# The second layer's ConvFFN in two phases: up by seven of eight quarter products, gated values through DRAM, down summed in PSUM

## The chip, the cores and the metric

One core of one Trainium2 chip. The metric is the device time of one execution in microseconds, the median of several runs. The engines are named as in the profile: PE is TensorE (matmul), DVE is VectorE, ACT is ScalarE, POOL is GpSimd, SP is SyncE, which issues most of the transfers.

## What is computed

A diffusion backbone of two layers over 1024 latent tokens and 256 context tokens, width 1024. Layer 0 mixes by differential attention and a Fourier mixer, layer 1 by Mamba-2 SSD and S5; every layer ends with a gated ConvFFN and a post-norm. The change is in the ConvFFN of layer 1, which works on the 1024 latent tokens alone. Cut from the reference:

```python
D_MODEL, SEQ, D_FF, CONV_K = 1024, 1024, 2816, 3
def conv_ffn(u, w_up, b_up, conv_w, conv_b, w_down, b_down):
    hdn = dwconv_centered(u @ w_up + b_up, conv_w, conv_b)   # 3 taps along the tokens
    val, gate = jnp.split(hdn, 2, axis=-1)
    return (val * jax.nn.silu(gate)) @ w_down + b_down
def post_norm_layer(h, y_mix, mods, ln_g, ln_b, ffn):
    h = layer_norm(ALPHA * h + mods[2][:, None] * y_mix, ln_g[0], ln_b[0])
    f = conv_ffn(modulate(h, mods[3], mods[4]), *ffn)
    return layer_norm(ALPHA * h + mods[5][:, None] * f, ln_g[1], ln_b[1])
```

## The kernel before

Every float32 operand of a matmul is split into a high part `h` (ACT, a copy into the fp32r type) and a low part `l` = value - high (DVE). A product of two operands takes three matmuls: high by high, high by low, low by high. `uh` and `ul` are the parts of the modulated input, channels on partitions, all 1024 tokens wide, made tile by tile by the output projection `out_proj` (L1304) that ends layer 1's mixer (`ul` at L372).

The hidden channels are worked on in NFB = 22 blocks `fb` of 128, each with a value half and a gate half (`conv_ffn`, L1466). Per block, PE does 2 halves x 2 token chunks x 8 k-blocks x 3 = 96 up matmuls of 128x512 (`up_mul`, L1426, into banks `mm`). ACT copies each bank with the bias into a padded row buffer `hb` (L1520). The convolution is one ACT instruction for the middle tap (L1540) and two DVE instructions for the outer ones (L1541, L1542), 1024 wide. Gating is a silu on ACT (L1546), a product on DVE (L1548) and the split of the result (L1552, L1554).

The down product runs one block behind: while PE does block `fb`'s gate half, the 48 down matmuls (L1561) of block fb - 1 are woven in, three up and three down in turn. Each group of three fills a bank (`tr` or `bg`), for one tile of 128 tokens and one half of the output width, and a DVE addition (L1575) adds the bank to `y` in SBUF: 16 additions per block. The down weights are multiplied by the residual gate on POOL when they arrive (L1500). The last three blocks' down products (`hold` = 3) are left to the tail: nine matmuls per bank, added by L2621, followed by the layer norm of each tile (L2609 to L2650) and the store of the output.

All of this is written out by hand in program order; each engine's queue is in that order. `FirstBlock` (L1430) reads the first block's weights ahead, and its product is begun inside `out_proj`. Loads of weights are issued by SP, two halves ahead (L1488, L1498). Beside it, POOL makes the residual from `yacc`, which stays in SBUF (L2582 to L2592).

## Time and profile before

| | |
|---|---|
| median of 3 runs | 3225.18 us (3224.17 to 3227.72) |
| span of the profiled execution | 3222.3 us |
| mean granted clock of TensorE in it | 0.978 |
| busy in the span: PE / DVE / ACT / POOL | 3056.3 / 2197.5 / 1207.7 / 743.2 us |
| layer 1's ConvFFN in it | from about 2431 us to the end |

The profile page gives, for one profiled execution, the busy time of each engine, the span in 40 slices, the chain of work that ended last, and the costliest groups of instructions. It names no other time of that execution than its span, from the first to the last instruction. Of the trace behind it, the windows give the same sums for any stretch, the timeline gives single instructions, and the chain of waits shows at each moment which work the end was waiting for.

### The profile page before, as it was taken

To read this page: it belongs to the slowest core of one execution; us is meant where nothing else is said; L and a number is where in the kernel's file an instruction comes from. 1 tells how busy PE (TensorE), PEld (TensorE's weight loads), DVE (VectorE), ACT (ScalarE), POOL (GpSimd) and SP (SyncE) were. 2 spreads that over 40 slices of the span, in tenths; PEclk is the share of its full clock that TensorE was granted. 3 is DMA by queue.
4 is the path that set the end of the run, shared out by engine and by line. 5 is a ranking of instruction groups with operands and counts; after the bars stand their busy time and mean duration, and the time that the engine had idled before them with its cause. 6 is when DMAs were issued, how large, how long until landed. Compare 5 with 4: busy or idle time off the path is not lost.

```text
span 3222.3 us, 39551 instructions
## 1 busy us (share of the span) xinstructions
PE 3056.3 (95%) x15416; PEld 2464.6 (76%) x15416; DVE 2197.5 (68%) x3214; ACT 1207.7 (37%) x2022; POOL 743.2 (23%) x639
## 2 busy tenths in 40 slices
PE   8999989999999999999999799997798999999997
PEld 4777779998888778877878577876487777777775
DVE  2288768886566565566666866759886667666667
ACT  3411258784522222222222452444354232232334
POOL 1056412221000000002430522216635301010013
PEclk9999999999999999999999899998899999999998
DMA  8635666613322222222321323320312121111111
GB/s 274 211 107 172 193 172 162 153 33 129 131 79 79 73 67 91 79 79 79 115 94 53 107 87 106 87 68 1 130 53 72 40 66 46 40 53 46 40 60 58
DMA packets 269614, 304.82 MB, mean 95 GB/s; under 512 B 22439, under 2 KB 206165, under 8 KB 269428
## 3 DMA queue, kind: packets, MB, share of 16 engines
q1 hardware_dynamic: 256452, 263.98, 26.8%
q0 software_dynamic: 6912, 23.11, 2.1%
q10 hardware_dynamic: 6064, 15.21, 1.6%
q8 instruction: 121, 1.98, 0.3%
q14 instruction: 65, 0.53, 0.1%
HBM read 237.48 MB, written 58.47 MB: 92 GB/s over the span
## 4 chain that ended last, share of the span: by engine, by line
PE 74%; DVE 16%; DMA 4%; ACT 3%; issue 2%; SPq 0%; POOL 0%; ACTq 0%; DVEq 0%; POOLq 0%
PE mm L1428 30%; PE tr L1561 10%; PE mm L1353 6%; PE bg L1561 5%; PE mm L2288 4%; PE s L1094 3%; PE mm L978 3%; PE mm L878 3%; PE bg L1152 3%; DVE cv L1542 2%; PE bg L266 1%; DVE cv L1541 1%; PE bg L1131 1%; PE tr L352 1%; PE bg L1817 1%
## 5 line engine op out<-in xcount | busy, mean ns | idle before, releaser
L1428 PE MATMUL mm<-uh,wusl 128*128 128x512 f32 (+1 forms) x1768 | 653.7, 370 | 7.6 <-DVE wusl L90 7.6
L1428 PE MATMUL mm<-uh,wush 128*128 128x512 f32 (+1 forms) x1768 | 655.4, 371 | 3.5 <-ACT wush L89 3.5
L1428 PE MATMUL mm<-ul,wush 128*128 128x512 f32 (+1 forms) x1768 | 654.6, 370 | 0.2 <-DVE ul L372 0.2
L1520 ACT ACTIVATE hb<-mm,ffc 128x512 f32<-128x512 f32 (+1 forms) x220 | 141.0, 641 | 975.3 <-PE mm L1428 975.2
L1575 DVE TENSOR_TENSOR y<-y,tr 128x512 f32<-128x512 f32 x469 | 317.4, 684 | 250.3 <-PE tr L1561 249.5
L1428 PEld LDWEIGHTS mm<-uh,wush 128*128 128x128 f32 x1768 | 333.8, 189 | 90.1 <-issue 23.6
L1428 PEld LDWEIGHTS mm<-uh,wusl 128*128 128x128 f32 x1768 | 333.8, 189 | 66.6 <-DVE wusl L90 10.2
L1428 PEld LDWEIGHTS mm<-ul,wush 128*128 128x128 f32 x1768 | 333.6, 189 | 64.7 <-DVE ul L372 0.4
L1575 DVE TENSOR_TENSOR y<-y,bg 128x512 f32<-128x512 f32 x235 | 160.8, 684 | 139.7 <-PE bg L1561 139.6
L1561 PE MATMUL tr<-wdsh,gh 128*128 128x512 f32 x516 | 209.0, 405 | 20.5 <-DVE y L1575 15.1
L1561 PE MATMUL tr<-wdsl,gh 128*128 128x512 f32 x516 | 204.4, 396 | 4.0 <-DVE wdsl L90 4.0
L1561 PE MATMUL tr<-wdsh,gl 128*128 128x512 f32 x516 | 205.8, 399 | 0.0
L1500 POOL TENSOR_TENSOR wdf<-wdf,g 128x1024 f32<-128x1024 f32 x22 | 68.4, 3108 | 573.9 <-DMA wdf<-in_ffn_w_down_dram 356.9
L1102 DVE TENSOR_REDUCE mx<-s 128x1 f32<-128x1280 f32 x120 | 150.6, 1273 | 47.7 <-PE s L1094 47.7
L1541 DVE SCALAR_TENSOR_TENSOR cv<-hb,ffc,cv 128x1282 f32<-128x1282 f32 (+3 forms) x91 | 134.4, 1477 | 48.1 <-ACT cv L1540 47.9
L1542 DVE SCALAR_TENSOR_TENSOR cv<-hb,ffc,cv 128x1282 f32<-128x1282 f32 (+3 forms) x91 | 163.8, 1800 | 3.5
L1659 POOL DMA_DIRECT2D g<-in_ln_g_dram x1 | 0.6, 599 | 623.0 <-DVE y L1575 623.0
L90 DVE TENSOR_TENSOR wusl<-wuf,wush 128x1024 fp32r<-128x1024 f32 x86 | 117.4, 1365 | 25.5 <-ACT wush L89 25.1
L1107 ACT ACTIVATE p<-s,mx 128x1280 f32<-128x1280 f32 x96 | 127.8, 1331 | 18.2 <-DVE r L1112 12.7
L1561 PEld LDWEIGHTS tr<-wdsh,gh 128*128 128x128 f32 x516 | 98.0, 190 | 47.8 <-DVE y L1575 22.8
L978 PE MATMUL mm<-uh,wsh 128*128 128x512 f32 (+1 forms) x320 | 124.8, 390 | 0.0
L1152 PE MATMUL bg<-vt,wt 128*128 128x128 f32 x960 | 124.5, 276 | 0.0
(694 smaller groups left out, 6720.3 us busy)
## 6 DMA issues: line engine op xcount, KB each, us to landing
wuf<-in_ffn_w_up_dram SPq DMA_DIRECT2D x88, 512.0 KB
adaw<-in_ada_w_dram SPq DMA_DIRECT2D x40, 1024.0 KB
wdf<-in_ffn_w_down_dram SPq DMA_DIRECT2D x44, 512.0 KB
wf<-in_attn_w_in_dram SPq DMA_DIRECT2D x18, 512.0 KB
adaw<-in_ada_w_dram SPq DMA_DIRECT2D x16, 512.0 KB
tq<-qd SPq DMA_DIRECT2D x24, 320.0 KB
t1k<-kd SPq DMA_DIRECT2D x24, 320.0 KB
t2k<-kd SPq DMA_DIRECT2D x24, 320.0 KB
```

The costliest lines, as they stand in the source:

```text
L978: T.matmul(pt.rearrange("p (t n) -> p t n", n=P), lhsT=w_[:, k, :], rhs=u_[:, o // P:(o + n) // P, k, :], start=(k + i == 0), stop=(k == K ...
L1102: V.reduce_max(t.mx[:, i, q:q + 1], t.s[i][:, c0:c0 + nk], axis=X, negate=True)
L1107: S.activation(t.p[i][q], t.s[i][:, c0:c0 + nk], AF.Exp, bias=t.mx[:, i, q:q + 1], accum_out=t.sm[:, i, q:q + 1])
L1152: T.matmul(t.po[:, P:2 * P], lhsT=t.wt[0][:, b, :], rhs=vt[:, b, :], start=(b == 0), stop=(b == NTT - 1))
L1353: T.matmul(pt, lhsT=u_[:, k, :], rhs=w_[k][:, hc], start=(k + i == 0), stop=(k == K - 1 and i == 2))
L1428: T.matmul(pt, lhsT=w_[:, k, :], rhs=u_[:, k, o:o + n], start=(k + j == 0), stop=(k == KB - 1 and j == 2))
L1520: S.activation(hb[vi][:, pos(o):pos(o) + n], pt[:, :n], AF.Identity, bias=ffc[l][:, 0, blk(b):blk(b) + 1])
L1541: V.scalar_tensor_tensor(out=c, in0=hb[vi][:, lo:hi], scalar=fc[:, 2], in1=c, op0=ALU.mult, op1=ALU.add)
L1542: V.scalar_tensor_tensor(out=c, in0=hb[vi][:, lo + 2:hi + 2], scalar=fc[:, 4], in1=c, op0=ALU.mult, op1=ALU.add)
L1561: T.matmul(pt, lhsT=g_[:, c0:c0 + P], rhs=w_[:, hc], start=(start and j == 0), stop=(stop and j == 2))
L1575: V.tensor_tensor(out=yacc[ti][:, hc], in0=yacc[ti][:, hc], in1=pt, op=ALU.add)
L2288: T.matmul(pt[0:M, :n], lhsT=w_[:, k, :], rhs=u_[:, k, o:o + n], start=(k + i == 0), stop=(k == KB - 1 and i == len(pairs) - 1))
```

## The change

Only layer 1's ConvFFN and its neighbours change; layer 0 still uses `conv_ffn`.

**Up phase** (`lat_up`). For one block of channels the up product is seen as a 2 x 2 matrix of quarters: rows are the value and the gate half of the weights, the inner index the two halves of the 1024 input channels, columns the two halves of the tokens. `a11` to `a22` are the quarters of the weights, `b11` to `b22` those of the input. Instead of eight quarter products (12 matmuls each) seven are made, in Winograd's form, from `s1` to `s4` (sums of weight quarters, made per block on DVE) and `t1` to `t4` (sums of input quarters, made once by `gen_sums`, t1 in the place of b12). Part of the recombination happens in PSUM, where a bank is read by ACT (`snap`) and then accumulated further, part by four DVE additions from PSUM into `hb` (`add`). Blocks 0 and 1 are still made plainly, with 96 matmuls each, while `gen_sums` works; the 20 others take 84. The gated values are not split: they are stored to DRAM as float32 (`g1_d`, 512 KB per block) from POOL's queue.

**Down phase** (`Down`). It begins when the up phase has ended. Four tiles of tokens by two halves fill all eight PSUM banks and all 22 blocks are accumulated there; then the same for the other four tiles. A step of this loop (one block, one group) is 24 matmuls. For each step SP loads the gated values (256 KB) and the down weights (512 KB, now read twice in all and not multiplied by the gate), two steps staged; ACT and DVE split both into one of five operand slots. At the end of a group the last three blocks are done bank by bank, and `tile_done` multiplies the bank by the gate, adds it to the residual and runs the layer norm. The normed stream `z` that the residual needs is stored to DRAM by `out_proj` and read back on POOL's queue; POOL makes the residual during the down phase.

Layer 1's `FirstPair` takes the place of `FirstBlock` (value and gate weights of block 0, split on POOL). The matmuls of this ConvFFN are 2 x 96 + 20 x 84 + 1056 = 2928, and were 22 x 96 + 1056 = 3168.

```diff
+    class FirstPair:
...
+        def product(self, ci, uh, ul):
+            o, n = self.chunks[ci]
+            pt = pp.tile([P, 512], F32, name='mm', bufs=4)
+            self.pts.append(pt)
+            for j, nm in enumerate(('a11', 'a12')):
+                quarter(pt[:, :n], self.hl[nm], [t[:, 4 * j:4 * j + 4, o:o + n] for t in (uh, ul)], j == 0, j == 1)
+
+    def quarter(pt, w, u, start, stop, step=lambda: None):
+        for k in range(4):
+            for j, (w_, u_) in enumerate(((w[0], u[0]), (w[0], u[1]), (w[1], u[0]))):
+                T.matmul(pt, lhsT=w_[:, k, :], rhs=u_[:, k, :], start=start and k + j == 0, stop=stop and k == 3 and (j == 2), skip_group_check=True)
+            step()
+
+    def lat_up(l, uh, ul, c0, pre, g_d, gq, plain, dpool, ones_ahead):
...
+        def summed(n, nm):
+            if n < NFB and n not in plain:
+                x, y, f = {'s1': ('a21', 'a22', ALU.add), 's2': ('s1', 'a11', ALU.subtract), 's3': ('a11', 'a21', ALU.subtract), 's4': ('a12', 's2', ALU.subtract)}[nm]
+                A[n, nm] = rpool.tile([P, 4, P], F32, name='s', bufs=3)
+                V.tensor_tensor(out=A[n, nm], in0=src(n, x), in1=src(n, y), op=f)
...
+        def gated(n):
+            if n >= 0:
+                V.tensor_tensor(out=cv[n, 0], in0=cv[n, 0], in1=cv.pop((n, 1)), op=ALU.mult)
+                gq(out=g_d[n], in_=cv.pop((n, 0)))
...
+        for n in range(len(plain), NFB):
...
+            X, Wb, Y, Z = [bank() for _ in range(4)]
+            quarter(X, w['a11'], U['b11'], True, True)
+            snap(n, 0, 0, X)
+            hi(m, 'a11')
+            silu(n - 1)
+            load(n + 2)
+            quarter(Wb, w['a12'], U['b21'], True, True)
+            lo(m, 'a11')
+            gated(n - 1)
+            summed(m, 's1')
+            hi(m, 'a12')
+            add(0, 0, Wb)
+            quarter(X, w['s2'], U['t2'], False, True)
...
+            snap(n, 0, 1, X)
...
+            quarter(Y, w['s1'], U['t1'], True, True)
...
+            snap(n, 1, 1, Y)
...
+            quarter(X, w['s3'], U['t3'], False, True)
...
+            snap(n, 1, 0, X)
+            hi(m, 's3')
+            add(1, 1, X)
...
+            quarter(Y, w['s4'], U['b22'], False, True)
+            lo(m, 's3')
+            add(0, 1, Y)
+            hi(m, 's4')
+            tap(n, 0)
...
+            quarter(Z, w['a22'], U['t4'], True, True)
+            lo(m, 's4')
+            conv(n, 0)
+            hi(m, 'a22')
+            add(1, 0, Z)
+            tap(n, 1)
+            lo(m, 'a22')
+            conv(n, 1)
...
+    class Down:
...
+        def load(self):
...
+                s = self.st[q] = [self.pool.tile([P, D], F32, name='wdf', bufs=2), self.pool.tile([P, 512], F32, name='gf', bufs=2)]
+                dma(out=s[1][:, :nt * P], in_=self.g_d[fb][:, t0 * P:(t0 + nt) * P])
+                dma(out=s[0], in_=a['ffn_w_down'][self.l, fb * P:(fb + 1) * P, :])
...
+        def run(self, bank, tile_done, step=lambda: None):
+            q = 0
+            for gi, (t0, nt) in enumerate(self.groups):
+                pts = [bank(i) for i in range(2 * nt)]
+                for fb in range(NFB - self.hold):
+                    for i in range(2 * nt):
+                        self.mul(pts[i], q, i // 2, i % 2, fb == 0, False)
+                        if i == 0 and self.ns < q + len(self.slots):
+                            self.load()
+                            self.split()
+                        step()
+                    q += 1
+                for i in range(2 * nt):
+                    for h in range(self.hold):
+                        self.mul(pts[i], q + h, i // 2, i % 2, False, h == self.hold - 1)
...
+                    tile_done(t0 + i // 2, i % 2, pts[i])
+                q += self.hold
...
-    out_proj(1, list(range(2, NTT)), NCTX, None, load_h2, (woh, wol), uh, ul, m3s, m3b, None, scale_g, None, pre, early, own=yacc)
+    out_proj(1, list(range(2, NTT)), NCTX, None, load_h2, (woh, wol), uh, ul, m3s, m3b, z_d, scale_g, None, pre, early, own=yacc)
...
-        conv_ffn(1, uh, ul, 8, [(0, 512), (512, 512)], [(0, 1024, 1)], yacc, pA, pB, pre, 3, fold=gate, bg=gen_res1(), nbg=9, dbank=dbank, ends=ends, begin=start)
+        dn = Down(1, g1_d, [(0, 4), (4, 4)], 3)
...
+        starter, finish_up, left = lat_up(1, uh, ul, 0, pre, g1_d, nc.gpsimd.dma_start, (0, 1), dpool, None)
+        finish_up()
...
+        dn.slots += [(p2, i) for i in range(2, 5)]
...
+        def tile_done(ti, half, pt):
+            h, hc = (hs[ti], slice(half * 512, half * 512 + 512))
+            V.tensor_tensor(out=pt, in0=pt, in1=gate[:, hc], op=ALU.mult)
+            V.scalar_tensor_tensor(out=h[:, hc], in0=h[:, hc], scalar=1.0, in1=pt, op0=ALU.mult, op1=ALU.add, accum_out=st2[half][:, ti:ti + 1])
```

How the queues change. PE in the middle of the ConvFFN, before: up products (`mm`) and down products (`tr`, `bg`) in turn, the down bank waiting for the DVE addition that frees it.

```order
L1428 MATMUL mm<-uh,wush 128x512
L1428 MATMUL mm<-ul,wush 128x512
L1428 MATMUL mm<-uh,wusl 128x512
L1561 MATMUL tr<-wdsh,gh 128x512 [waits DVE_49]
L1561 MATMUL tr<-wdsl,gh 128x512
L1561 MATMUL tr<-wdsh,gl 128x512
L1428 MATMUL mm<-uh,wush 128x512
```

And now, in a short block, where the third quarter product ends and the fourth begins (L1478 is `quarter`; `t2h` is the high part of t2):

```order
L1478 MATMUL mm<-t2h,s2h 128x512
L1478 MATMUL mm<-t2l,s2h 128x512
L1478 MATMUL mm<-t2h,s2l 128x512
L1478 MATMUL mm<-uh,s1h 128x512 [waits DVE_49]
L1478 MATMUL mm<-ul,s1h 128x512
L1478 MATMUL mm<-uh,s1l 128x512
L1478 MATMUL mm<-uh,s1h 128x512
```

No down product stands between them, and the only wait is at the head of a quarter.

DVE in a block before (`y` additions, the convolution `cv`, the split of weights):

```order
L1548 TENSOR_TENSOR cv_22261<-cv_22261,cv_22382 128x1024 [waits Activation_49]
L1554 TENSOR_TENSOR gl<-cv_22261,gh 128x1024 [waits Activation_49]
L90 TENSOR_TENSOR wusl<-wuf,wush 128x1024 [waits DMAHW3_49,Activation_49]
L1575 TENSOR_TENSOR y_18199<-y_18199,tr 128x512 [waits PE_49] x2
L1575 TENSOR_TENSOR y_18200<-y_18200,bg 128x512 [waits PE_49]
L1541 SCALAR_TENSOR_TENSOR cv_22478<-hb_20292,ffc_101,cv_22478 128x1024 [waits Activation_49]
L1542 SCALAR_TENSOR_TENSOR cv_22478<-hb_20292,ffc_101,cv_22478 128x1024 [waits DVE_49]
```

And now, in a short block (`s1l` to `s4l` are low parts of the next block's sums, `hbv` and `hbg` the row buffers, L1562 the additions from PSUM, L1544 the convolution):

```order
L1534 TENSOR_TENSOR s1l<-s,s1h 128x512 [waits PE_49,Activation_49]
L1522 TENSOR_TENSOR s<-wuv,s 128x512 [waits DVE_49]
L1562 TENSOR_TENSOR hbg<-hbg,mm 128x512 [waits Activation_49]
L1534 TENSOR_TENSOR s3l<-s,s3h 128x512 [waits PE_49,Activation_49]
L1562 TENSOR_TENSOR hbv<-hbv,mm 128x512 [waits PE_49]
L1534 TENSOR_TENSOR s4l<-s,s4h 128x512 [waits Activation_49]
L1544 SCALAR_TENSOR_TENSOR cvv<-hbv,ffc_101,cvv 128x1024 [waits DMASW7_49,Activation_49]
L1544 SCALAR_TENSOR_TENSOR cvv<-hbv,ffc_101,cvv 128x1024 [waits DVE_49]
L1562 TENSOR_TENSOR hbg<-hbg,mm 128x512 [waits PE_49]
L1534 TENSOR_TENSOR a22l<-wug,a22h 128x512 [waits Activation_49]
L1544 SCALAR_TENSOR_TENSOR cvg<-hbg,ffc_101,cvg 128x1024 [waits Activation_49]
L1544 SCALAR_TENSOR_TENSOR cvg<-hbg,ffc_101,cvg 128x1024 [waits DVE_49]
```

The additions into `y` are gone; each block has small instructions for the next block's operands between those for its own recombination.

DVE in the second plain block, in the middle of `gen_sums` (`xb`, `xt`, `t4l` are its work; `s1l` and `a22l` here are the low parts of that block's gate weights):

```order
L1589 TENSOR_TENSOR t4l<-xb_20474,t4h 128x512 [waits Activation_49]
L1574 TENSOR_TENSOR xb_20496<-uh,ul 128x512
L1574 TENSOR_TENSOR xb_20501<-uh,ul 128x512 [waits DVE_49]
L1577 TENSOR_TENSOR xt_20503<-xb_20501,xb_20496 128x512 [waits DVE_49]
L1574 TENSOR_TENSOR xb_20509<-uh,ul 128x512
L1534 TENSOR_TENSOR s1l<-wug,s1h 128x512 [waits DMAHW4_49,PE_49,Activation_49]
L1534 TENSOR_TENSOR a22l<-wug,a22h 128x512 [waits PE_49,Activation_49]
L1544 SCALAR_TENSOR_TENSOR cvg<-hbg,ffc_101,cvg 128x1024 [waits Pool_49]
L1544 SCALAR_TENSOR_TENSOR cvg<-hbg,ffc_101,cvg 128x1024 [waits DVE_49,Pool_49]
```

`s1l` is the 42nd instruction of DVE after the last `ul` of the output projection; PE's gate half of the second plain block (L1478, `mm<-uh,s1l`) waits for it.

## Rows read from the trace of the kernel before

**Rows 1.** The page: busy time of each engine, and GB/s in 40 slices of the span.

```profile
PE 3056.3 (95%) x15416; PEld 2464.6 (76%) x15416; DVE 2197.5 (68%) x3214; ACT 1207.7 (37%) x2022; POOL 743.2 (23%) x639
...
GB/s 274 211 107 172 193 172 162 153 33 129 131 79 79 73 67 91 79 79 79 115 94 53 107 87 106 87 68 1 130 53 72 40 66 46 40 53 46 40 60 58
```

**Rows 2.** Windows: stretch, length, busy us (instructions) PE, PEld, DVE, ACT, POOL; PEclk, DMA share, GB/s.

```profile
2345.00:2440.00 95.00, 94.36 (x466) 77.45 (x465) 76.01 (x166) 52.86 (x108) 40.02 (x18) 1.00 0.19 64
...
2700.00:2800.00 100.00, 97.69 (x423) 78.79 (x422) 68.52 (x73) 28.79 (x32) 9.94 (x3) 1.00 0.15 48
3160.00:3222.00 62.00, 40.88 (x166) 32.03 (x164) 52.09 (x128) 26.31 (x35) 24.14 (x10) 0.84 0.17 68
```

**Rows 3.** Chain of waits, late and at the last block: start us, us, what.

```profile
2692.84 3.30 DVE cv L1542
...
3101.96 3.29 DVE cv L1542
...
3119.40 21.80 PE mm L1428 x96
```

**Rows 4.** Timeline of PE: alternating products, then after an idle time.

```profile
2703.16 0.39 PE L1428 MATMUL mm<-uh,wush 128*128 128x512 f32 x1
...
2704.55 0.39 PE L1428 MATMUL mm<-uh,wush 128*128 128x512 f32 x1
...
2473.27 0.80 PE L1428 MATMUL mm<-uh,wusl 128*128 128x512 f32 x1 [3.24 <-DVE wusl L90]
...
2480.57 0.63 PE L1428 MATMUL mm<-ul,wush 128*128 128x512 f32 x1
2480.99 0.63 PE L1428 MATMUL mm<-uh,wusl 128*128 128x512 f32 x1
```

**Rows 5.** Timeline of DVE from 2709 to 2734: start us, us, what.

```profile
2712.95 1.28 DVE L1542 SCALAR_TENSOR_TENSOR cv<-hb,ffc,cv 128x1024 f32<-128x1024 f32 x1
2715.36 1.23 DVE L1548 TENSOR_TENSOR cv<-cv,cv 128x1024 f32<-128x1024 f32 x1 [1.13 <-ACT cv L1546]
...
2727.29 3.29 DVE L1542 SCALAR_TENSOR_TENSOR cv<-hb,ffc,cv 128x1024 f32<-128x1024 f32 x1
2730.51 0.67 DVE L1575 TENSOR_TENSOR y<-y,tr 128x512 f32<-128x512 f32 x1
2731.11 0.68 DVE L1575 TENSOR_TENSOR y<-y,bg 128x512 f32<-128x512 f32 x1
```

**Rows 6.** Timeline of POOL, same stretch.

```profile
2726.18 3.33 POOL L1500 TENSOR_TENSOR wdf<-wdf,g 128x1024 f32<-128x1024 f32 x1 [31.13 <-DVE y L1575]
```

**Rows 7.** Groups by line from 2400 to the end: count, busy us, mean ns, idle before.

```profile
L1575 DVE TENSOR_TENSOR y<-y,tr 128x512 f32<-128x512 f32 x203 | 136.1, 682 | 94.1 <-PE tr L1561 94.1
...
L1561 PE MATMUL tr<-wdsh,gh 128*128 128x512 f32 x236 | 97.7, 414 | 20.5 <-DVE y L1575 15.1 <-DVE y L2621 5.5
...
L1520 ACT ACTIVATE hb<-mm,ffc 128x512 f32<-128x512 f32 x88 | 60.2, 685 | 408.9 <-PE mm L1428 408.9
```

**Rows 8.** Timeline of DVE in the last 60 us.

```profile
3200.35 0.20 DVE L2630 TENSOR_SCALAR tst<-tst,tst 128x1 f32<-128x1 f32 x1
...
3205.49 0.20 DVE L2630 TENSOR_SCALAR tst<-tst,tst 128x1 f32<-128x1 f32 x1
...
3209.21 0.08 DVE L2621 DVE_READ_ACCUMULATOR y<-y,tr 128x1 f32 x1
```

**Rows 9.** Chain of waits at the start of the second ConvFFN.

```profile
2441.90 0.70 DVE ul L372
...
2444.99 10.74 PE mm L1428 x46
```

**Rows 10.** SP's queue, then instructions and landing of tile gl (POOL's queue).

```profile
2720.91 0.57 SPq L1498 DMA_DIRECT2D wdf<-in_ffn_w_down_dram  x1
...
L2576 POOL DMA_DIRECT2D gl<-in_ln_b_dram x1: 536/536/536, 2437.1 to 2437.1; - x1
...
DMA to landing us min/median/max: 4.8/4.8/4.8
```

More of the change, by code (lines that the diff above doesn't have):

```diff
@@ L2547, in load_h2 @@
     def load_h2(t, tt):
+        hc = [slice(0, 512), slice(512, D)]
         if not ln2:
-            ln2.extend([bc_row(pre.pool, a['ln_g'][0, 1:2, :], "wush"), bc_row(pre.pool, a['ln_b'][0, 1:2, :], "wusl")])
-        g2, b2 = ln2
+            for i, rows in enumerate((a['ln_g'], a['ln_b'])):
+                for j in range(2):
+                    ln2.append(pre.pool.tile([P, 512], F32, name=f"a1{j + 1}{'hl'[i]}"))
+                    dma(out=ln2[-1], in_=rows[0, 1:2, hc[j]].broadcast_to([P, 512]))
         dma(out=t, in_=z2_d[tt * P:(tt + 1) * P, :])
-        G.tensor_tensor(out=t, in0=t, in1=g2, op=ALU.mult)
-        G.tensor_tensor(out=t, in0=t, in1=b2, op=ALU.add)
+        for j in range(2):
+            G.tensor_tensor(out=t[:, hc[j]], in0=t[:, hc[j]], in1=ln2[j], op=ALU.mult)
+            G.tensor_tensor(out=t[:, hc[j]], in0=t[:, hc[j]], in1=ln2[2 + j], op=ALU.add)
     def scale_g(ot, tt):
@@ new lines, in body, with dpool, load_z, resid @@
+    g1_d = dp.tile([NFB, P, NLAT], F32, name="g1d")
+    with tc.manual_schedule():
+        dn = Down(1, g1_d, [(0, 4), (4, 4)], 3)
+        def dpool():
+            dn.guard = tc.tile_pool(name="dn1", bufs=1)
+            return dn.start()
+        starter, finish_up, left = lat_up(1, uh, ul, 0, pre, g1_d, nc.gpsimd.dma_start, (0, 1), dpool, None)
+        finish_up()
+        phf.close()
+        ph4.close()
+        dn2 = tc.tile_pool(name="dm1", bufs=1, side="right")
+        p2 = dn2.__enter__()
+        dn.slots += [(p2, i) for i in range(2, 5)]
+        epg = tc.tile_pool(name="ep1", bufs=1, side="right")
+        ep = epg.__enter__()
+        gate, g1, r, g2, b2 = [ep.tile([P, D], F32, name=nm) for nm in ("gate", "g1", "r", "g2", "b2")]
+        for t, src in ((gate, mods_d[1][1:2, 5 * D:6 * D]), (r, a['ffn_b_down'][1:2, :]), (g1, a['ln_g'][1, 0:1, :]), (g2, a['ln_b'][1, 0:1, :]), (b2, a['ln_b'][1, 1:2, :])):
+            nc.gpsimd.dma_start(out=t, in_=src.broadcast_to([P, D]))
+        hs = {}
+        def load_z(t):
+            if t < 8 and t not in hs:
+                hs[t] = ep.tile([P, D], F32, name="z", bufs=5)
+                nc.gpsimd.dma_start(out=hs[t], in_=z_d[(t + 2) * P:(t + 3) * P, :])
+        def resid(t):
+            G.tensor_tensor(out=hs[t], in0=hs[t], in1=g1, op=ALU.mult)
+            yield
+            G.tensor_tensor(out=hs[t], in0=hs[t], in1=r, op=ALU.add)
+            yield
+        def gen_resid():
+            for t in range(5):
+                load_z(t)
+            G.tensor_scalar(gate, gate, IALPHA, None, ALU.mult)
@@ L2594, in gen_res1 @@
-            for t, src in ((g2, a['ln_g'][1, 1:2, :]), (b2, a['ln_b'][1, 1:2, :])):
-                dma(out=t, in_=src.broadcast_to([P, D]))
-                yield
-        first = []
-        ends = {}
-        conv_ffn(1, uh, ul, 8, [(0, 512), (512, 512)], [(0, 1024, 1)], yacc, pA, pB, pre, 3, fold=gate, bg=gen_res1(), nbg=9,
-                 dbank=dbank, ends=ends, begin=start)
-        last = ends['down']
-        junk = pB.tile([P, D], F32, name="wdf")
-        st2 = [pB.tile([P, 8], F32, name=f"tst{i}") for i in range(5)]
+            G.tensor_tensor(out=r, in0=r, in1=g2, op=ALU.add)
@@ L2604, in body @@
+            nc.gpsimd.dma_start(out=g2, in_=a['ln_g'][1, 1:2, :].broadcast_to([P, D]))
+            yield
+            for t in range(5):
+                yield from resid(t)
+        st2 = [ep.tile([P, 8], F32, name=f"tst{i}") for i in range(5)]
         chain = Drip(V)
```

336 lines of the change are left out of this document (282 added, 54 removed).

## The prediction

> **What bounds the kernel now.** I read the page's busy shares first, then the windows by stage, then the chain of waits inside the second layer's ConvFFN, then single instructions. The page says that TensorE is busy for 95% of the span [rows 1]. The window over a steady stretch of this stage says the same more sharply: 97.69 of 100 us, at full granted clock, while VectorE is at 68.52, ScalarE at 28.79, and the transfers move 48 GB/s [rows 2]. So the stage is paced by the number of matmuls times their pitch. The pitch comes from the chain: 96 matmuls in 21.80 us are 0.227 us each [rows 3]. Where up and down products alternate by threes, six starts take 1.39 us, 0.232 each [rows 4].
>
> What lies above that is small. The chain passes through the same long convolution step once per block of channels, at 2692.84 and, 12 blocks later, at 3101.96 [rows 3]: 409.12 / 12 = 34.09 us per block, of which 144 matmuls at 0.2267 us are 32.64. Of the missing 1.45 us a third is the mixed pitch; the rest is the down product's bank that waits for VectorE's add, while VectorE sits in a 3.29 us instruction beside POOL's 3.33 us fold [rows 5, 6]; the same form takes 1.28 us alone [rows 5]. These waits are most of the 15.1 us of idle time that the lines put on the adds [rows 7]. The end is different: in the last 62 us TensorE is busy for 40.88, clock 0.84, and VectorE for 52.09 [rows 2]. There the layer norm of each tile sets the pace, 3205.49 - 3200.35 = 5.14 us per tile [rows 8].
>
> **The change, part by part.** By the listing of instructions nothing differs before the end of layer 1's output projection. From there I go by four stages, on the clock of the span, 3222.3 us; the median of the runs lies 2.9 us above it and I add that at the end.
>
> *Removed.* 240 matmuls (20 blocks of 84 in place of 96), 240 x 0.2267 = 54.4 us of the busiest engine. Also 304 adds of layer 1's down products on VectorE (16 in each of 19 blocks), 0.68 us each [rows 7], and POOL's 22 folds. Most of those adds lay beside matmuls and give nothing directly; the 1.45 us per block goes, but only to be replaced by what is late next.
>
> *Stage 1, two plain blocks.* 192 matmuls, but VectorE must now form t1 to t4. After the last column of the input is there (VectorE's last `ul` ends at 2442.6, the first long run of matmuls starts at 2444.99 [rows 9]) TensorE has 24 matmuls of half width (2.7 us) and 72 whole ones (16.3 us), and reaches the gate half of the second plain block at 2464.0. This half needs `s1l`, the 42nd VectorE instruction from there in the order: 40 of 512 columns at 0.60 us back to back (2730.51 to 2731.11) and two convolution steps at 1.31 (1.28 and the gap to the next) [rows 5]. That is 26.6 us, so 2469.2 with no waits at all; several of them wait for a ScalarE conversion of 0.69 us [rows 7], for which I add 5 us: 2474.4. At 0.69 us apart and with the same handoffs it would be 2478. So TensorE stalls for about 10 us. After an idle 3.24 us the trace shows a pitch of 0.42 us [rows 4] for the 13 recorded matmuls that follow, 13 x 0.20 = 2.6 us lost, so I charge 3.6 after a longer stall. The 72 matmuls left take 16.3, and 1.5 us come from the output projection, where a weight conversion on ScalarE now stands ahead of the last tiles' work (two of its 0.69 us instructions). 2474.4 + 3.6 + 16.3 + 1.5 = **2496** for the start of the 20 short blocks (2484 without the stall, 2500 at the slow end).
>
> *Stage 2, 20 blocks of seven quarter products.* TensorE needs 84 x 0.2267 = 19.04 us, or 19.46 at the mixed pitch of 0.2317. VectorE has 15 instructions of 512 columns (four sums, seven low parts, four adds from PSUM), the gating multiplication (1.23) and four convolution steps (1.31): 15 x 0.62 + 1.23 + 5.24 = 15.8 us busy [rows 5]. It also waits twice for ScalarE, once for the convolution's first tap after the last quarter and once for the silu, 2.7 us together. That is 18.5 of 19.04 us: TensorE still sets the pace, with about 1 us to spare. ScalarE has 11 conversions and snapshots of 0.685 [rows 7] and three of twice the width, under 12 us. The loads are 1 MB of weights and the store 0.5 MB per block, 1.57 MB / 19.4 us = 81 GB/s, against 274 in the first slice of the span [rows 1]. I take 19.4 us: 20 x 19.4 = 388, the stage ends at **2884**. The gated values must be stored before the next block's tap writes the same buffer; the store has some 8 us for that, and a transfer of this size from POOL's queue landed in 4.8 [rows 10].
>
> *Stage 3, the down products.* 1056 matmuls, all accumulated in PSUM, at 0.229 (the middle of both pitches) = 241.8 us. A step is 24 matmuls, 5.5 us. In it VectorE makes two low parts (0.62 + 1.23), ScalarE two high ones, POOL one residual instruction; even the 2 us that POOL added to a VectorE step [rows 5, 6] fits. A step loads 0.79 MB, 143 GB/s, three times the 48 of before [rows 2]. The trace of before has no such steady load here, so I bound it: nothing if the 274 GB/s of the first slice hold [rows 1], 1.6 to 2.6 us per step if the rate stays at 97 to 111 GB/s, as in several slices of before, or each transfer takes what `wdf` took, issued at 2720.91 and used at 2726.18 [rows 6, 10]. I take nothing, since staging runs two steps ahead. Two transitions cost: at the start, 5 rows and 5 tiles (5.2 MB) come in on POOL's queue beside the first steps, and three of five operand slots become free only with the last up matmul, 8 us; between the groups, the eight banks become free only as VectorE finishes each tile (6.3 us per tile, below, against TensorE's 18 x 0.229 = 4.1), 8 us. Each could be 0 to 15.
>
> *Stage 4, the end.* Before, the tail had eight tiles, now four. VectorE does two more instructions of 0.6 us per tile than in the 5.14 us cadence [rows 8], 6.3 us. The last three steps' matmuls (72, 16.5 us) lie inside: 2 + 4 x 6.3 + 13 = 40 us from their first to the end, where 13 is the present distance from the last sum at 3209.2 to 3222.3 [rows 8].
>
> **Sum:** 2884 + (241.8 - 16.5) + 8 + 8 + 40 = 3165.3 against 3222.3, and with 2.9 us outside the span **3168 us**. Beside the 54 us of matmuls the old waits go (21 x 1.45 = 30 us and what the first block lost), and stage 1's stall, the two transitions and the pitch take most of that back.
>
> **The rivals.**
> *VectorE paces stage 2.* Speaking for it: only about 1 us to spare per block, and a chain of handoffs with ScalarE in which each side can be late. If its 512-column instructions take 0.69 (alone) rather than 0.62 and the handoffs 4.7 rather than 2.7 us, a block takes 21.5 us: 20 x 2.1 = 42 us more, **3210**. Against it: in before it drains bursts at 0.60 [rows 5], and POOL, the cause of its long instructions, computes nothing here.
> *No waits at all.* Pitch 0.2267 everywhere, stage 1's stall hidden, 4 us at the transitions: **3134**. For it: steady windows of 98% [rows 2]. Against it: 41 instructions ahead of one that TensorE needs.
> *Loads bound stage 3,* the case on the other side. Mechanism: staging holds two steps, each of two transfers on one queue, and a step's load waits for the split that frees its buffer. At 7.2 to 8.1 us per step in place of 5.5 the 44 steps cost 75 to 114 us, **3243 to 3282**. My forecast has 57 us to give, 57 / 44 = 1.3: it decides from 6.8 us per step, 116 GB/s. For it: no slice of before after the second moves more than 193 GB/s [rows 1]. Against it: low rates of before are low demand, and a load has two steps' time.
> *The stores on POOL's queue are late.* If a store takes 10 us or more and not 4.8, the tap waits, and with it convolution and snapshots: 2.1 us x 20, **3210** as well. The Trainium skill speaks for this one (SBUF — State Buffer, Who interferes with whom): transfers issued from GpSimd can starve while VectorE runs in its two-port modes, and such transfers should go to another queue. By this page the stores of stage 2 would be late and the time near 3210; the page excepts tensor_tensor, the bulk of VectorE's work here. The rows speak against: one from POOL's queue, issued at 2437.1, landed in 4.8 us in a stretch where VectorE was busy for 76.01 of 95 us [rows 2, 10].
>
> **How the numbers follow.** My forecast, 3150 to 3185 around 3168, has 0.66; VectorE's pace 0.15; no waits 0.10; late stores 0.03; loads 0.06. The range 3140 to 3212 leaves out the loads, half of the no-wait case and about half of the two cases near 3210, some 0.2. A measurement can tell about 0.2% (6.5 us) from no change, so faster means under 3218.7: everything but the loads and the upper edge of VectorE's pace. Faster 0.91, the same 0.03, slower 0.06.
>
> **What would show it.** Right: in the steady part of the short blocks TensorE's starts of equal quarters lie 19.0 to 19.6 us apart, with VectorE above 80% busy; a stall of 7 to 12 us at `s1l` in the second plain block, then slow matmuls; 44 steps of 5.4 to 5.6 us with no wait for staging; a hole under 15 us between the groups. Wrong: quarter products that wait for VectorE in every block (first rival), an idle TensorE ended by conversions that follow a transfer in stage 3 (third), taps that wait for the store (fourth), or a boundary between the groups that costs 20 us or more.

## The result, and the profile after

The changed kernel took 3149.9 us (median of 4 runs, 3147.91 to 3151.14) against 3226.45 for the kernel before in the same runs: a ratio of 0.9765, 95% interval 0.9751 to 0.9779. The forecast was 3168 within 3140 to 3212. The profiled execution has a span of 3148.6 us. The head of its page (as in [rows 1]):

```profile
span 3148.6 us, 39836 instructions
...
PE 2989.8 (95%) x15176; PEld 2420.1 (77%) x15176; DVE 2202.4 (70%) x3281; ACT 1277.2 (41%) x2179; POOL 689.7 (22%) x664
```

TensorE is still busy for 95%, but with 66.5 us less work (3056.3 before [rows 1]). The windows by stage (columns as in [rows 2]) are the first 29 us of stage 1, the middle of the short blocks, and the down phase:

```profile
2441.00:2470.00 29.00, 18.47 (x87) 15.00 (x85) 28.05 (x42) 9.60 (x16) 0.00 (x0) 0.87 0.07 19
2700.00:2800.00 100.00, 100.00 (x437) 81.76 (x436) 81.26 (x104) 52.71 (x73) 2.66 (x5) 1.00 0.26 84
2860.00:2960.00 100.00, 95.99 (x413) 78.11 (x412) 71.73 (x48) 36.89 (x45) 45.38 (x26) 0.98 0.63 214
2960.00:3060.00 100.00, 94.99 (x406) 77.41 (x405) 67.28 (x102) 36.60 (x48) 24.62 (x12) 0.97 0.51 170
```

At the start VectorE is at work for 28.05 of 29 us. In the short blocks TensorE is never idle, 100.00 of 100, where it was 97.69 before, and VectorE is at 81.26 instead of 68.52. The transfers, 48 GB/s before in the same stretch [rows 2], are at 84 now, and at 170 to 214 in the down phase. The stages can be read off single starts of TensorE (timeline: start us, us, instruction, idle time before it and its releaser):

```profile
2459.26 0.39 PE L1478 MATMUL mm<-uh,a12l 128*128 128x512 f32 x1
2472.47 0.79 PE L1478 MATMUL mm<-uh,s1h 128*128 128x512 f32 x1 [12.82 <-ACT s1h L1529]
...
2476.02 0.39 PE L1478 MATMUL mm<-uh,s1l 128*128 128x512 f32 x1
...
2496.08 0.39 PE L1478 MATMUL mm<-t2h,s2h 128*128 128x512 f32 x1
...
2862.40 0.39 PE L1478 MATMUL mm<-t2h,s2h 128*128 128x512 f32 x1
...
2876.20 0.39 PE L1766 MATMUL mm<-wdh,gh 128*128 128x512 f32 x1
...
2882.05 0.72 PE L1766 MATMUL mm<-wdh,gh 128*128 128x512 f32 x1 [3.61 <-DVE hbg L1562]
```

*Stage 1.* TensorE reaches the gate half of the second plain block at 2459.5, waits 12.82 us, and works slowly until 2476.02: eight matmuls at a pitch of 0.43 us instead of 0.227, with a granted clock of 0.50 from 2470 to 2475, the lower of its two levels (1.2 of 2.4 GHz). The last 3 us of the wait are ScalarE's: behind a conversion that VectorE's work releases at 2469.41 its queue still holds the copy of a bank and a convolution step, and only then `s1h`, at 2471.80. *Stage 2.* The third quarter product begins at 2496.08 in the first short block and at 2862.40 in the last, so a block takes 366.32 / 19 = 19.28 us. *Stage 3.* The first down matmul starts at 2876.20; after nine matmuls TensorE waits 3.61 us for a bank. From the first short block to the end, these are all its waits (who waits, for whom, us, times, longest):

```profile
PE bg L1766 <- DVE z L2990: 3.7, 2, 1.9
PE mm L1766 <- DVE hbg L1562: 3.6, 1, 3.6
PE tr L1766 <- DVE z L2990: 1.3, 1, 1.3
PE mm L1766 <- DVE wdl L1746: 0.4, 1, 0.4
```

And the chain of waits at the end (start us, us, what; the matmuls, then VectorE at the first bank of the second, third and fourth tile):

```profile
3114.53 6.13 PE mm L1766 x27
3120.68 0.71 DVE mm L2989
...
3126.42 0.62 DVE tr L2989
...
3132.07 0.62 DVE bg L2989
```

It begins with the first 27 of the 72 matmuls that finish the last group. At 2.04 us a bank (9 x 0.227) they would be done at 3114.53 + 16.3 = 3130.9; VectorE follows at 5.7 us per tile (3126.42 - 3120.68, 3132.07 - 3126.42), with the end at 3148.6.

One more reading is needed before runs are compared. The instructions up to this layer's output projection are the same in all of them (in the changed kernel and its variants up to the end of it), yet the last `ul` there starts between 2437 and 2449 us. In the changed kernel it is this row:

```profile
2440.87 0.69 DVE L372 TENSOR_TENSOR ul<-utmp,uh 128x512 fp32r<-128x512 f32 x1 [1.37 <-ACT uh L370]
```

So beside the medians I count from this instruction, the anchor, to the end of the span: 3148.6 - 2440.87 = 707.7 us, and before 3222.3 - 2441.90 = 780.4 [rows 9]. The change is 72.7 us there. This count has a scatter of its own: stretches that a run does not touch still differ by up to 1.9 us between runs (from the first down matmul to the end 271.06 us in e2_sums_half and 272.92 in e1_plain21), partly by the number of slow matmuls after the same wait. I read differences under 2 us as none.

### The profile page after: what moved, and what is told of

It is laid out like the page before. It is cut to its first block, busy times and chain, and to the rows that moved or that the text cites. A ratio compares the mean times of both kernels' runs of the same rounds, so it can differ in the third digit from the quotient of the medians.

```text
span 3148.6 us, 39836 instructions
## 1 busy us (share of the span) xinstructions
PE 2989.8 (95%) x15176; PEld 2420.1 (77%) x15176; DVE 2202.4 (70%) x3281; ACT 1277.2 (41%) x2179; POOL 689.7 (22%) x664
## 4 chain that ended last, share of the span: by engine, by line
PE 75%; DVE 14%; DMA 5%; ACT 3%; issue 2%; SPq 0%; POOL 0%; DVEq 0%; ACTq 0%; POOLq 0%
PE mm L1428 18%; PE mm L1478 13%; PE tr L1902 6%; PE mm L1353 6%; PE mm L2629 4%; PE bg L1902 3%; PE s L1094 3%; PE mm L878 3%; PE mm L1766 3%; PE bg L1152 3%; PE mm L978 2%; PE bg L266 1%; PE bg L1131 1%; PE bg L1766 1%; PE tr L1766 1%
## 5 line engine op out<-in xcount | busy, mean ns | idle before, releaser
L1428 PE MATMUL mm<-uh,wush 128*128 128x512 f32 (+1 forms) x1056 | 378.6, 358 | 0.0
L1428 PE MATMUL mm<-uh,wusl 128*128 128x512 f32 (+1 forms) x1056 | 374.8, 355 | 3.2 <-DVE wusl L90 3.2
L1428 PE MATMUL mm<-ul,wush 128*128 128x512 f32 (+1 forms) x1056 | 375.5, 356 | 0.0
L1916 DVE TENSOR_TENSOR y<-y,tr 128x512 f32<-128x512 f32 x266 | 181.3, 686 | 153.1 <-PE tr L1902 152.3
L1428 PEld LDWEIGHTS mm<-uh,wush 128*128 128x128 f32 x1056 | 199.4, 189 | 57.3 <-issue 23.6
L1428 PEld LDWEIGHTS mm<-ul,wush 128*128 128x128 f32 x1056 | 199.4, 189 | 35.2
L1428 PEld LDWEIGHTS mm<-uh,wusl 128*128 128x128 f32 x1056 | 199.2, 189 | 32.9 <-DVE wusl L90 4.0
L1152 PEld LDWEIGHTS bg<-vt,wt 128*128 128x128 f32 x960 | 116.6, 193 | 0.7
L978 PE MATMUL mm<-ul,wsh 128*128 128x512 f32 (+1 forms) x320 | 115.1, 360 | 0.0
L978 PE MATMUL mm<-uh,wsl 128*128 128x512 f32 (+1 forms) x320 | 114.9, 359 | 0.0
```

The costliest lines, as they stand in the source:

```text
L978: T.matmul(pt.rearrange("p (t n) -> p t n", n=P), lhsT=w_[:, k, :], rhs=u_[:, o // P:(o + n) // P, k, :], start=(k + i == 0), stop=(k == K ...
L1152: T.matmul(t.po[:, P:2 * P], lhsT=t.wt[0][:, b, :], rhs=vt[:, b, :], start=(b == 0), stop=(b == NTT - 1))
L1428: T.matmul(pt, lhsT=w_[:, k, :], rhs=u_[:, k, o:o + n], start=(k + j == 0), stop=(k == KB - 1 and j == 2))
L1916: V.tensor_tensor(out=yacc[ti][:, hc], in0=yacc[ti][:, hc], in1=pt, op=ALU.add)
```

## The experiments

| run | median, us | last `ul` starts | span | from there to the end | against 707.7 |
|---|---|---|---|---|---|
| e1_plain21 | 3200.97 | 2437.01 | 3195.6 | 758.6 | +50.9 |
| e2_sums_half | 3151.16 | 2443.73 | 3151.7 | 708.0 | +0.3 |
| e3_three_plain | 3148.54 | 2443.65 | 3148.3 | 704.7 | -3.0 |
| e4_hold5 | 3147.33 | 2442.18 | 3146.2 | 704.0 | -3.7 |
| e5_dve4 | 3182.72 | 2445.81 | 3182.2 | 736.4 | +28.7 |
| e6_double_load | 3147.59 | 2439.43 | 3147.2 | 707.8 | +0.1 |
| e7_store_sp | 3157.8 | 2442.82 | 3156.5 | 713.7 | +6.0 |
| e8_banks | 3151.58 | 2443.10 | 3151.1 | 708.0 | +0.3 |
| e9_split_first | 3142.84 | 2440.42 | 3139.3 | 698.9 | -8.8 |
| e10_sums_pool | 3158.53 | 2439.63 | 3154.7 | 715.1 | +7.4 |
| e11_all | 3135.7 | 2449.10 | 3141.3 | 692.2 | -15.5 |

**What the seven quarter products are worth.**

```diff
-        ... = lat_up(1, uh, ul, 0, pre, g1_d, nc.gpsimd.dma_start, (0, 1), dpool, None)
+        ... = lat_up(1, uh, ul, 0, pre, g1_d, nc.gpsimd.dma_start, tuple(range(21)), dpool, None)
```

> Two phases without quarter products: 21 blocks of channels made plainly (96 matmuls), only the last with seven quarter products. 19 blocks x 12 = 228 matmuls come back. My theory (the matmul count is what stage 2 is worth, the two phases alone win back the old waits of 1.45 us per block): 228 x 0.2267 = 51.7 us above the changed kernel's 3149.9, so 3198 to 3206, still below 3226. Rival (the seven quarter products bring little because VectorE's sums eat it, and the gain is the phases'): 3150 to 3170. Second rival (the phases bring nothing): 3222 to 3230.

Measured: 3200.97 us (ratio to before 0.9921, 0.9901 to 0.9941), 50.9 us more from the anchor. The 228 matmuls cost 0.223 us each, nearly all of their pitch of 0.227, and the two phases without quarter products are still faster than before. Both rivals fall. The window over its middle shows the plain blocks without any idle time too:

```profile
2600.00:2800.00 200.00, 200.00 (x879) 164.84 (x878) 82.91 (x85) 74.06 (x101) 4.79 (x9) 1.00 0.23 72
```

So the two phases give the part that is not matmuls, about 22 us net of what stage 1 and the transitions cost (2.7 of them are the 12 matmuls that the one short block saves), and the quarter products the rest. In such a window before, TensorE was idle for 2.3 of 100 us [rows 2], with waits for the additions [rows 7]; how much of the 22 us these waits make and how much the mixed pitch, no run separates.

**Stage 1: the stall.** First its order: `gen_sums` advances at every second step only in block 0.

```diff
-            step = lambda: next(sums, None)
+            calls = [0]
+
+            def step():
+                calls[0] += 1
+                if calls[0] > 24 or calls[0] % 2 == 0:
+                    next(sums, None)
```

> The forming of t1 to t4 is stepped half as fast in block 0, so that less of it stands ahead of the second plain block's gate weights; the same work in all. If only the order is at fault, the 12.8 us stall in stage 1 goes with the slow matmuls behind it: 3133 to 3137. If VectorE's amount of work in stage 1 sets the start of the short blocks (53.62 busy of the 60 us from 2440 to 2500), the stall only moves to the first short block: 3146 to 3152. I lean to the second.

Measured: no gain. The stall moved, whole, to the first short block's first weights, as expected:

```profile
2492.24 0.79 PE L1478 MATMUL mm<-uh,a11h 128*128 128x512 f32 x1 [13.28 <-ACT a11h L1529]
...
2497.52 0.62 PE L1478 MATMUL mm<-uh,a12h 128*128 128x512 f32 x1
```

Then more matmuls to cover the same work, three plain blocks (and half the pace up to the 56th step):

> Three plain blocks and t1 to t4 formed at half the pace over them: 12 matmuls more (2.7 us). If VectorE's backlog is what the stall is made of, all of it is hidden now: 12.8 us of stall and about 3.6 us of slow matmuls go, 2.7 come: 3134 to 3138. If the backlog was not the cause (the gate weights' transfer or conversion is late by itself), 3152 to 3154.

Measured: 3.0 us less, not 13. Two of the terms were wrong. The stall did not go whole: 1.79 and 2.98 us are left, and a plain block brings convolution and gating of its own to VectorE (2.61 us from 2482.31, 1.22 from 2470.47). And slow matmuls came twice:

```profile
2480.67 0.50 PE L1478 MATMUL mm<-uh,a11h 128*128 128x512 f32 x1 [1.79 <-ACT a11h L1529]
...
2482.51 0.63 PE L1478 MATMUL mm<-uh,a11h 128*128 128x512 f32 x1
...
2485.07 0.63 PE L1478 MATMUL mm<-uh,a12h 128*128 128x512 f32 x1
...
2491.26 0.50 PE L1478 MATMUL mm<-uh,s1h 128*128 128x512 f32 x1 [2.98 <-ACT s1h L1529]
```

Here seven matmuls have a pitch of 0.43 us, from 2482.51 to 2485.07 (granted clock 0.50 from 2482.5 to 2485.5), after an idle time of only 1.79 us, and eight more follow the 2.98 us; in the changed kernel eight matmuls were slow after 12.82 us, in the run before it thirteen after 13.28 us. But in the seven other runs that keep this wait at 12.81 to 12.84 us, 7 to 14 follow it, so such a number can't be put down to the idle time. What these runs show is that a wait of 1.79 us can cost as many slow matmuls as one of 12.82.

Last, VectorE's work itself: the 16 additions that restore the input go to POOL.

```diff
-                    V.tensor_tensor(out=x[nm], in0=fr(U[nm][0])[:, k, :], in1=fr(U[nm][1])[:, k, :], op=ALU.add)
+                    G.tensor_tensor(out=x[nm], in0=fr(U[nm][0])[:, k, :], in1=fr(U[nm][1])[:, k, :], op=ALU.add)
```

> The 16 additions of 512 columns that give the input back from its two parts are made on POOL, which is idle in stage 1, and no longer on VectorE. From the last low part of the input to the end (707.7 in the changed kernel): if VectorE's amount of work is what makes the stall of 12.8 us, 16 x 0.6 = 9.6 us go from it and the time is 697 to 701. Rival (POOL's instruction takes 1.5 us or more per 512 columns, 3.1 per 1024 before, and lengthens VectorE's beside it, as 1.28 became 3.29 before): 707 to 716.

Measured: 7.4 us slower, all of it ahead of the short blocks; the stall is 19.9 us instead of 12.8. The rival is right. POOL needs 1.57 us for what VectorE does in 0.6, and VectorE's own instructions of 512 columns become 1.8 us where they meet one, against 0.69 (2478.97) alone. By group, then by start:

```profile
L1574 POOL TENSOR_TENSOR xb<-uh,ul 128x512 f32<-128x512 f32 x16 | 24.7, 1569 | 24.4 <-DVE ul L372 12.5 <-DVE t1f L1581 8.2 <-DVE t2l L1588 3.7
```

```profile
2451.93 1.78 DVE L1534 TENSOR_TENSOR a11l<-wuv,a11h 128x512 fp32r<-128x512 f32 x1
...
2478.97 0.69 DVE L1534 TENSOR_TENSOR s1l<-wug,s1h 128x512 fp32r<-128x512 f32 x1 [3.07 <-ACT s1h L1529]
```

All three together: the stall follows the time that VectorE (with ScalarE's handoffs) needs for this work. Spreading it shortens the stall, reordering only moves it, and POOL makes it worse.

**Stage 2: how far is VectorE from pacing it?**

```diff
...
             conv(n, 1)
+            for _ in range(4):
+                V.tensor_tensor(out=junk, in0=hb[1][:, 1:513], in1=hb[1][:, 513:1025], op=ALU.add)
```

> Each of the 20 short blocks gets four more VectorE instructions of 512 columns at its end, into an unused bank (extra work, the output is as before): 4 x 0.69 = 2.8 us. Theory of the prediction (VectorE has 18.5 of 19.28 us taken, its 3.6 us of waits per block being mostly handoffs that stay): the period becomes 21 us, 20 x 1.8 to 2.0 = 36 to 40 us more, 3186 to 3190. Rival (all of its 3.6 us of idle time are spare, TensorE is far ahead): 3148 to 3154.

Measured: 3182.72 us, +28.7 from the anchor, between what the theory and the rival expected: 23.0 of it in the short blocks, where I had put 36 to 40. TensorE now waits in 18 of the 20 short blocks, and again at the start of the down phase, since the bank that I used is one of that phase's:

```profile
PE mm L1478 <- ACT hbg L1559: 18.5, 18, 1.1
...
PE tr L1769 <- DVE tr L1714: 5.0, 1, 5.0
```

```profile
2600.00:2800.00 200.00, 189.64 (x817) 152.32 (x816) 176.77 (x236) 97.01 (x137) 5.32 (x10) 1.00 0.24 77
```

VectorE's busy time per block went from 0.8126 x 19.28 = 15.67 us to 18.1 (0.8839 x the new period). The period comes from the same kind of start as above: the third quarter begins at 2501.39 in the first short block and at 2890.74 in the last; 389.35 / 19 = 20.49. Work of 2.44 us more per block made the period 1.21 longer: 1.2 us per block were to spare and no more, though VectorE was idle for 3.6. VectorE's waits from 2500 to 2860 say which part that was. In the changed kernel two of the five are

```profile
DVE hbv L1562 <- PE mm L1478: 13.5, 18, 0.8
...
DVE cvv L1552 <- ACT cvg L1548: 10.0, 19, 0.5
```

together 1.3 us per block, the wait for TensorE's bank and the one for the silu. In this run they are 0.4 and 0.5 us in all. The other three, for the first taps and for `s2h` on ScalarE, stay: 40.9 us in the changed kernel and 37.9 here.

**Stage 3: are the loads near their bound?**

```diff
+                if 8 <= q < 40:
+                    x = self.again[q % 4]
+                    dma(out=x, in_=a['ffn_w_down'][self.l, fb * P:(fb + 1) * P, :])
...
```

> In 32 of the 44 steps of the down phase SP issues two more transfers, 512 and 256 KB, of the same weights into unused DRAM (extra work, the output is as before): 1.57 MB per step of 5.44 us, 289 GB/s. Theory (staging runs two steps ahead and the transfers have room; at the start of the phase they reached 408 GB/s): 3148 to 3156. Rival (the loads were close to the bound, and a step follows them): 7 us per step, 32 x 1.6 = 50 us more, 3200.

Measured: no difference, 707.8 from the anchor, with 294 GB/s over 100 us in which the changed kernel moves 170:

```profile
2960.00:3060.00 100.00, 95.69 (x410) 77.95 (x409) 60.91 (x101) 35.97 (x45) 17.57 (x10) 0.97 0.79 294
```

The loads are far from their bound, and the rival on the slower side falls. What the prediction feared at 111 GB/s is not a ceiling: in slices of 5 us from 2860 on, the changed kernel moved

```profile
GB/s 200 220 49 166 102 25 281 408 399 408 407 191 139 157 109 139 214 171 300 202 276 218 173 124 79 0 155 143 22 0 51 102 324 339 277 223 306 229 215 140
```

**Stage 3: who issues the stores.**

```diff
-        ... = lat_up(1, uh, ul, 0, pre, g1_d, nc.gpsimd.dma_start, (0, 1), dpool, None)
+        ... = lat_up(1, uh, ul, 0, pre, g1_d, dma, (0, 1), dpool, None)
```

> The stores of the gated values are issued by SP and not by POOL. Theory (a store has 8 us and lands in 2.9): 3147 to 3153, no difference. Rival (issuing from POOL beside a busy VectorE costs, as the prediction's fourth rival has it): over 5 us less, under 3145. A third way: a store that waits in SP's queue for the gating holds up the weights behind it, 3155 or more.

Measured: 6.0 us slower from the anchor, and not in stage 2, where the period stays 19.28 us; 5.0 of it come behind the first down matmul, the other 1.0 in stage 1, which the edit does not touch. It is the third way: in SP's queue the last blocks' stores, which wait for the gating, stand ahead of the first loads of the down phase. The first `gf` transfer is issued at 2869.35, right behind the store at 2868.85, and at 2860.18 in the changed kernel, 7.2 us later when both are counted from the last `ul`. TensorE's waits for operands in stage 3, 0.4 us in the changed kernel, become 3.6, and eight slow matmuls follow the longest:

```profile
PE mm L1766 <- DVE wdl L1746: 3.6, 3, 2.9
```

In the changed kernel a store from POOL's queue landed in 2.9 us (section 6 of its page, KB and median us at the end):

```profile
g1d<-cvv POOLq DMA_DIRECT2D x22, 512.0 KB, 2.9
```

The Trainium skill (SBUF — State Buffer, Who interferes with whom) says that a transfer issued from GpSimd can starve beside VectorE's two-port modes and should then go to another queue, and excepts tensor_tensor, the bulk of VectorE's work here. With VectorE busy for 81%, no run shows a starved store, and moving it cost time.

**Stage 3: the start.** The banks that the up phase does not use first:

```diff
-        banks = [('mm', 4)] * 4 + [('tr', 2)] * 2
+        banks = [('tr', 2)] * 2 + [None] * 2 + [('mm', 4)] * 4
...
```

> Only the order in which the down phase takes its eight banks is changed: the four that the up phase does not use come first. Theory (the first of them that TensorE waits for, 3.6 us, is held by VectorE's last addition from PSUM, and slow matmuls follow): most of 3.6 us and some 2 us of slow matmuls go, 3143 to 3146. Rival (VectorE is late anyhow, the wait moves to the operands of the next steps): 3148 to 3152.

Measured: nothing. The wait for the bank went from 3.6 to 0.9 us, and 2.9 us of waits for `wdl` came in its place, as the rival had it:

```profile
PE mm L1766 <- DVE z L2990: 4.3, 3, 1.8
PE tr L1766 <- DVE wdl L1746: 2.9, 6, 1.0
PE mm L1766 <- DVE hbg L1562: 0.9, 1, 0.9
```

Its VectorE timeline says why. The longest of these waits, 1.0 us, is for the third step's operands (`gl`, `wdl`), which stand behind the gating of the last block, in order:

```profile
2889.57 1.23 DVE L1552 TENSOR_TENSOR cvv<-cvv,cvg 128x1024 f32<-128x1024 f32 x1 [1.13 <-ACT cvg L1548]
...
2891.32 1.22 DVE L1746 TENSOR_TENSOR wdl<-wdf,wdh 128x1024 fp32r<-128x1024 f32 x1
```

The other five, 0.3 to 0.4 us each and 6.16 us apart, come one per step from 2914.95 on, where POOL makes the residual. There VectorE's two splits, 0.69 and 1.22 us alone, take 2.91 and 3.43, and the same stretch of the changed kernel shows it too:

```profile
2917.70 3.28 POOL L2943 TENSOR_TENSOR z<-z,r 128x1024 f32<-128x1024 f32 x1
2918.62 2.91 DVE L1745 TENSOR_TENSOR gl<-gf,gh 128x512 fp32r<-128x512 f32 x1
2920.92 2.88 POOL L2941 TENSOR_TENSOR z<-z,g 128x1024 f32<-128x1024 f32 x1
2921.45 3.43 DVE L1746 TENSOR_TENSOR wdl<-wdf,wdh 128x1024 fp32r<-128x1024 f32 x1
```

So VectorE needs 6.2 us per step there, and TensorE 5.44.

Only the first of the two causes is a matter of order. So, with the other order of banks kept, I had the third step split ahead of the gating:

```diff
-        finish_up()
         phf.close()
...
         dn.slots += [(p2, i) for i in range(2, 5)]
+        dn.load()
+        dn.split()
+        finish_up()
...
```

> As the run with the other order of banks, and the third step's operands are split ahead of the last block's silu and gating, behind which they stood on ScalarE and VectorE. Counted from the last low part of the input to the end (707.7 us in the changed kernel, 708.0 with the order of banks alone). Theory (the 3.6 us wait at the start of the down phase was made of two things in VectorE's order, the addition that frees the bank and the operands behind the gating): both go, 702 to 704. Rival (the transfers of these steps, or POOL's rows beside them, are late by themselves): 706 to 709.

Measured: 698.9, 8.8 us less than the changed kernel and more than I expected. TensorE's waits in stage 3 fell from 9.0 us to 4.5:

```profile
PE tr L1766 <- DVE wdl L1746: 2.0, 4, 0.7
PE mm L1766 <- DVE z L2992: 1.6, 1, 1.6
PE mm L1766 <- DVE hbg L1562: 0.9, 1, 0.9
```

The waits between the groups (3.7 and 1.3 in the changed kernel) became 1.6 as well, which I had not expected; the order of banks alone left 4.3 there. VectorE's order at the end of the first group shows the reason. With the order of banks alone a split stands between the second and the third bank, and waits for ScalarE besides:

```profile
2997.51 0.69 DVE L1745 TENSOR_TENSOR gl<-gf,gh 128x512 fp32r<-128x512 f32 x1 [1.89 <-ACT gh L1743]
2998.45 1.23 DVE L1746 TENSOR_TENSOR wdl<-wdf,wdh 128x1024 fp32r<-128x1024 f32 x1 [0.26 <-ACT wdh L1744]
2999.60 0.69 DVE L2989 TENSOR_TENSOR bg<-bg,gate 128x512 f32<-128x512 f32 x1
```

Here one step more is split ahead from the start, so this pair is not there, and from VectorE's first bank to its third it takes 4.75 us (2984.88 to 2989.63) instead of 8.82 (2990.78 to 2999.60).

The other 4.3 of the 8.8 us are slow matmuls: the changed kernel has 8 from 2882.05 on and 13 from 3012.96 on, 21 x 0.2 = 4.2 us, with a granted clock of 0.93 and 0.92 in the windows around them. Here both windows have 1.00, and no wait of stage 3 is followed by slow matmuls; the same holds in e11_all below.

**Stage 4: the end.**

```diff
...
-        dn = Down(1, g1_d, [(0, 4), (4, 4)], 3)
+        dn = Down(1, g1_d, [(0, 4), (4, 4)], [3, 5])
```

> The second group of four tiles holds back five blocks instead of three for the end, so that PE needs 15 matmuls (3.4 us) per bank where VectorE needs 2.8. My theory (28 us from the last matmul to the end are VectorE's backlog of tiles, 15.7 us, and the last tile's own chain, 12.4): the backlog shrinks to about 2 us, 3135 to 3139. Rival (VectorE's chain ends when it ends, whatever PE does): within 3 us of 3149.9.

Measured: 3.7 us less, where I expected 11 to 15 and the rival under 3. My theory began with a misreading: 28 us from the last matmul to the end. The chain leaves TensorE at 3120.66 because VectorE is later from there on, not because TensorE has finished, which is at 3130.9. The backlog was 3136.25 - 3130.9, some 5 us, and not 15.7. It did go: VectorE now waits for each bank (3.4 us apart). But near the end one of its 1.28 us instructions took 3.02 us beside two additions of POOL (5.69 us):

```profile
3115.42 0.70 DVE L2990 TENSOR_TENSOR mm<-mm,gate 128x512 f32<-128x512 f32 x1 [1.72 <-PE mm L1766]
...
3118.82 0.70 DVE L2990 TENSOR_TENSOR mm<-mm,gate 128x512 f32<-128x512 f32 x1 [0.39 <-PE mm L1766]
...
3130.50 3.02 DVE L2978 SCALAR_TENSOR_TENSOR z<-z,tst,g 128x1024 f32<-128x1024 f32 x1
```

```profile
3130.03 5.69 POOL L2969 TENSOR_TENSOR z<-z,b 128x1024 f32<-128x1024 f32 x2 [64.17 <-ACT z L2968]
```

**All that helped, together** (three plain blocks, five held back, order of banks, early split):

> Three plain blocks, five blocks held back in the last group, the other order of banks and the early split together. Alone they gave, counted from the last low part of the input, -3.1, -3.7 and, for the last two, -4 to -6 if the theory holds: 707.7 - 11 to 13 = 695 to 697, some 3138 on the median. If the gains do not add (the end waits for the residual or the loads): 699 to 703.

Measured: 3135.7 us, ratio to before 0.9716 (0.9693 to 0.9739), and 692.2 from the anchor, 15.5 less than the changed kernel, and below the 695 to 697 expected, because the last two gave 8.8 and not 4 to 6: the gains of the parts, 3.0 + 3.7 + 8.8, add up. The median carries the anchor's own scatter (2449.10 in the profiled execution, the latest of all), so the difference from the anchor is the better number.

## Why the prediction was right, step by step

The direction and the bound of every stage were right: matmuls set the pace of stages 2 and 3, VectorE that of stages 1 and 4. The time was 18 us too high, in all four stages by the size of a term, and one of the terms was right in size only by luck. The 3149.9 us lie in the range, and 0.1 us below the 3150 to 3185 that had 0.66. Part of any such distance is the scatter ahead of the change; counted from the last `ul`, the forecast was 3165.3 - 2441.9 = 723.4 us and the result 707.7.

- **Stage 1** was to end at 2496 and ended at 2490.6 (2496.08 less two quarters of 2.72). The stall stood at the named half of the second plain block. It was 12.8 us and not 10, above the 7 to 12 that were given as the sign, because TensorE came there at 2459.5 and not at 2464: I counted from 2444.99 [rows 9], where the kernel before waited for a weight conversion that the change no longer has at this point; here the matmuls go on at 2441.62. That lengthens the stall and not the stage, whose end VectorE sets: from the end of the last `ul` (2441.56) to the end of the stall it is 30.9 us, and 31.8 in the forecast (2442.6 to 2474.4). The 5.4 us are 1.9 by which the stall ended earlier (1.0 of them because the last `ul` did), 1.9 of slow matmuls (some 1.7 us where I charged 3.6; the 13 of the kernel before that I went by follow waits of 2.70, 3.24 and 2.07 us and not one of 3.24), and the 1.5 us charged to the output projection, which can't be told from the scatter.
- **Stage 2** was 20 x 19.4 and is 20 x 19.28 = 385.6 us: 2.4 less, with VectorE at 81.26% where I gave over 80. "About 1 us to spare" is what e5_dve4 found, 1.2, so the first rival (0.15) was near: two VectorE instructions more per block would have begun to make it true.
- **Stage 3** was 241.3 us up to the last 72 matmuls and took 3114.53 - 2876.20 = 238.3. The pitch was 0.2267, the lower of the two that I averaged, which is 2.2 of the 3.0. The two transitions, 8 + 8, came out as 238.3 - 984 x 0.2267 = 15.2 us lost, 6.8 up to the first finished bank (VectorE takes it at 2988.45) and 8.4 behind it; 9.0 of them are waits. The second has the cause that I named, banks that VectorE frees tile by tile, with the splits in between as e9_split_first shows. The first is luck: I charged it to 5.2 MB of rows and tiles and to operand slots that come free late, and what TensorE waited for was a bank held by VectorE's last addition, 3.61 us, with eight slow matmuls behind it. And VectorE's step was mis-sized: I let it fit with 2 us more beside POOL, 3.9 of 5.5 us, but both splits are lengthened, to 6.2 us per step. In the changed kernel the operands made ahead cover that up to a wait of 0.4 us; e8_banks shows it as 1.9 us of waits.
- **Stage 4** was 40 us and took 34.1: 5.7 us per tile instead of 6.3, and 12.4 instead of 13 behind the last sum; and the first tile, which has no earlier one to finish beside it, took less than the others (3116.60 to 3120.68).
- The sum of the four differences is -5.4 - 2.4 - 3.0 - 5.9 = -16.7 us, which is 3165.3 - 3148.6. The rest of the 18 is the time outside the span, 1.3 us here and 2.9 in the forecast.
- **Rivals.** No waits at all (3134) was the direction in which I erred; stage 2 really has none. The loads (0.06) are excluded by e6_double_load. The late stores (0.03) are excluded by the 2.9 us in which they landed and the missing waits of stage 2; e7_store_sp shows that another queue gains nothing.
